# A two-layer decoder trunk on one core: ordering the whole program by a simulated timeline

## The chip, the core and the metric

The kernel runs on one core of a Trainium2 chip. It has a matrix engine (PE, whose weight loads are listed apart as PEld), a vector engine (DVE), a scalar engine (ACT), a general engine (POOL) and a queue that issues transfers (SP). Each engine works through its own list of instructions, and semaphores between the lists keep the data right. The metric is the time of one whole execution on the device in microseconds, the median of several runs.

## The reference

The input is one sequence of 512 tokens with 1024 channels, float32. Two layers each do a token mixer and a gated MLP, with a norm before each and a plain residual add; a last norm follows.

```python
def reference(x, ...):
    h = x
    for i in range(DEPTH):                       # DEPTH = 2
        hn = rms_norm(h, norm_mix[i])
        if i % N_MIXERS == 0:
            mix = pool_mixer(hn, pool_w[j], pool_b[j], pool_scale[j])
        else:
            mix = swa_sink_attention(hn, attn_w_qkv[j], attn_b_qkv[j], attn_sinks[j], attn_w_o[j])
        h = h + mix
        hn = rms_norm(h, norm_ffn[i])
        h = h + conv_glu_ffn(hn, ffn_w_in[i], ffn_conv_w[i], ffn_conv_b[i], ffn_w_out[i])
    return rms_norm(h, norm_f)
```

The pool mixer takes causal means over windows of 2, 4, 8 and 16 tokens, one window for each quarter of the channels, subtracts the token itself, and multiplies by one 256x256 matrix per quarter. The attention has 16 query heads of 64 over 4 key heads, a window of 128 tokens, a linear distance bias and one sink per head. The MLP goes from 1024 to 2x2816 channels, through a causal convolution of width 3 in each channel, multiplies one half by the silu of the other, and goes back to 1024.

## The kernel before

**Products.** Activations lie with channels on the 128 partitions and the 512 tokens along the row. Every product of the model is made three times on PE, from a rounded part (`_h`) and a rest (`_l`) of both factors: high by high (L84), high weight by low activation (L85), low weight by high activation (L86), in `mm3`. A weight tile is fetched by SP (L90, three raw buffers), rounded by a Copy on ACT (L98), and its rest is taken by a subtraction on DVE, in places on POOL (L101). There are four buffers each for `wh` and `wl`. PE adds up into eight banks, which are handed out in rings.

**Start, the pool mixer.** Tokens are squared on ACT (L268) and scaled on DVE (L270). 64 narrow matmuls with band matrices that POOL builds (L167 to L174) make the windowed means in all eight banks (L273). ACT reads a bank into `px_h` (L253), DVE takes the rest `px_l` (L254); this is `split_scaled`. Then come 48 products with the pool weights `wpool`. `h` arrives by transfer, gets a bias on ACT (L301) and the product on DVE (L307), and is split again into `f0x_h`, `f0x_l`, the input of the first MLP. Among the `px` splits the first MLP tiles, `wi_0_1`, `wi_0_0` and `wi_1_1`, get their Copy; their names give the index and the half of the gate.

**MLP.** Each MLP has two halves of 11 hidden tiles. `mlp_in` makes for each tile two banks of 24 matmuls, one for the value and one for the gate. The norm is not applied to the input; its reciprocal root is multiplied onto the product when DVE reads the bank (L315, `c_u`). So in the first half of each MLP the first banks wait for the norm. PE sums the squares (L232), DVE does the root, DVE puts it on a diagonal `n_d` (L242), PE spreads it over the partitions with a matmul by ones (L243), and ACT copies the result to `n_rb` (L246). Then follow the convolution (L318 to L320), silu (L344), the product `zz` (L347) and its split (L350, L351). `mlp_out` goes back by 33 matmuls for each of eight output tiles.

**Attention.** 16 units, one for each key head and block of 128 queries, go through scores (PE L556, DVE L559), the exponential (ACT L573), the scaling by the denominator (POOL L578), transposes (PE L586, split on ACT L589 and DVE L590) and the weighted values (PE L84 to L86 with `vh`, `vl`; split by ACT L605 and DVE L606). The source places fillers between these steps: the products of the later query tiles (`ax` by `kq`) and of the output projection (`o` by `wo`), at a set rate per unit.

**End.** The last norm is done in two token halves. The first half has its root spread by L243, copied (L246), and eight POOL multiplications (L689) make tiles `o` that SP sends out (L690). The second half is turned by PE (L664), its squares are summed (L699), and ACT and DVE scale four tiles `ob` (L715, L717) that SP sends out (L718).

**What sets the order.** The source is read once, and each instruction is recorded with what it depends on. A scheduler of the framework then makes each engine's list from this record. It chooses the next instruction by a model of the engines' times and respects the dependences, the buffers and the banks. The order in the source is only a starting point: where two instructions don't depend on each other they may stand either way round.

## Time and profile before

| | before |
|---|---|
| median of 3 runs | 929.1 us (928.81 to 929.13) |
| profiled execution | 929.16 us |
| its span | 927.4 us |
| granted PE clock, mean | 0.998 |
| PE busy | 913.8 us, 99% of the span |
| PEld busy | 770.3 us, 83% |
| DVE busy | 576.5 us, 62% |
| ACT busy | 423.3 us, 46% |
| POOL busy | 140.8 us, 15% |

The profile is of one execution. Rows of a timeline show the start, the duration, the engine, the line of the program, the operation, the output and its inputs, the shape, and in brackets how long the engine sat idle before it and what released it. Consecutive instructions of one kind on one engine stand in one row with their count. Matmuls are pipelined: the duration of one is longer than the distance from its start to the start of the next, and it is this distance that adds up.

### The profile page before, as it was taken

What the parts mean: (1) busy time and instruction counts of PE and PEld (TensorE: products, weight loads), DVE (VectorE), ACT (ScalarE), POOL (GpSimd) and SP (SyncE); (2) the same over time, 40 slices, a digit from 0 to 9 for tenths busy, and PEclk for the clock granted to TensorE, in tenths of its full rate; (3) what the DMA queues carried; (4) which work ended last, traced back from release to release, by engine and by line L of the source; (5) the groups of instructions that cost most, each with busy time, mean ns of one, the idle gap of its engine ahead of it and who ended that gap; (6) DMA issues with size and microseconds to landing.
All of it is one profiled execution on the core that took longest, in us unless ns stands there. A gap on an engine that the chain in (4) does not pass through costs nothing.

```text
span 927.4 us, 11708 instructions
## 1 busy us (share of the span) xinstructions
PE 913.8 (99%) x4419; PEld 770.3 (83%) x4419; DVE 576.5 (62%) x944; ACT 423.3 (46%) x682; POOL 140.8 (15%) x243
## 2 busy tenths in 40 slices
PE   8999999999999999999999999999999999999997
PEld 7788888888888888898888888888888888888896
DVE  5679776336777764455887472987743377677433
ACT  7655443223444443436887451744422244444532
POOL 9600000000000001227665140000000000000022
PEclk9999999999999999999999999999999999999999
DMA  9233222343222223322110041242233422322312
GB/s 332 70 113 114 91 86 76 97 128 111 94 92 93 77 77 98 133 92 91 47 46 24 18 142 51 86 150 95 63 94 100 136 91 93 110 80 63 96 61 91
DMA packets 28856, 88.14 MB, mean 95 GB/s; under 512 B 3200, under 2 KB 4352, under 8 KB 28800
## 3 DMA queue, kind: packets, MB, share of 16 engines
q1 hardware_dynamic: 28800, 87.40, 29.2%
q8 instruction: 34, 0.56, 0.3%
q14 instruction: 22, 0.18, 0.1%
HBM read 85.29 MB, written 2.10 MB: 94 GB/s over the span
## 4 chain that ended last, share of the span: by engine, by line
PE 91%; ACT 4%; DVE 2%; POOL 2%; issue 1%; ACTq 0%; POOLq 0%; DVEq 0%
PE bank L85 30%; PE bank L84 30%; PE bank L86 29%; ACT sc L573 1%; PE bank L556 1%; PE bank L586 1%; DVE tl L590 0%; ACT px_h L253 0%; POOL wo_l L101 0%; DVE q L469 0%; ACT th L589 0%; DVE sc L559 0%; PE bank L243 0%; ACT wi_h L98 0%; PE bank L273 0%
## 5 line engine op out<-in xcount | busy, mean ns | idle before, releaser
L226 POOL TENSOR_TENSOR n_acc<-n_acc,n_sq 128x512 f32<-128x512 f32 (+1 forms) x28 | 39.1, 1396 | 716.4 <-ACT n_sq L217 709.8
L98 ACT ACTIVATE wi_h<-wi_raw 128x1024 fp32r<-128x1024 f32 x88 | 92.9, 1060 | 109.1 <-PE bank L85 100.3
L85 PE MATMUL bank<-f0x_l,wi_h 128*128 128x512 f32 x352 | 137.1, 389 | 0.8 <-DVE f0x_l L254 0.8
L84 PE MATMUL bank<-f0x_h,wi_h 128*128 128x512 f32 x352 | 137.2, 390 | 0.0
L84 PE MATMUL bank<-f1x_h,wi_h 128*128 128x512 f32 x352 | 137.1, 390 | 0.0
L84 PE MATMUL bank<-zh,wo_h 128*128 128x512 f32 (+1 forms) x363 | 137.0, 378 | 0.0
L86 PE MATMUL bank<-f0x_h,wi_l 128*128 128x512 f32 x352 | 137.0, 389 | 0.0
L86 PE MATMUL bank<-f1x_h,wi_l 128*128 128x512 f32 x352 | 136.9, 389 | 0.0
L85 PE MATMUL bank<-f1x_l,wi_h 128*128 128x512 f32 x352 | 136.9, 389 | 0.0
L86 PE MATMUL bank<-zh,wo_l 128*128 128x512 f32 (+1 forms) x363 | 136.6, 376 | 0.0
L85 PE MATMUL bank<-zl,wo_h 128*128 128x512 f32 (+1 forms) x363 | 136.6, 376 | 0.0
L101 DVE TENSOR_TENSOR wi_l<-wi_raw,wi_h 128x1024 fp32r<-128x1024 f32 x84 | 102.7, 1225 | 48.9 <-ACT wi_h L98 37.2
L98 ACT ACTIVATE wo_h<-wo_raw 128x768 fp32r<-128x768 f32 (+1 forms) x70 | 57.5, 823 | 121.8 <-PE bank L85 109.9
L315 DVE TENSOR_TENSOR c_u<-bank,n_rb 128x512 f32<-128x512 f32 x88 | 60.0, 688 | 75.9 <-PE bank L86 75.9
L101 DVE TENSOR_TENSOR wo_l<-wo_raw,wo_h 128x768 fp32r<-128x768 f32 (+1 forms) x66 | 60.4, 915 | 54.5 <-ACT wo_h L98 54.3
L84 PEld LDWEIGHTS bank<-zh,wo_h 128*128 128x128 f32 x363 | 68.3, 188 | 12.4
L86 PEld LDWEIGHTS bank<-zh,wo_l 128*128 128x128 f32 x363 | 68.3, 188 | 12.3
L85 PEld LDWEIGHTS bank<-zl,wo_h 128*128 128x128 f32 x363 | 68.3, 188 | 12.3
L85 PEld LDWEIGHTS bank<-f0x_l,wi_h 128*128 128x128 f32 x352 | 66.1, 188 | 14.8 <-DVE f0x_l L254 1.2
L84 PEld LDWEIGHTS bank<-f0x_h,wi_h 128*128 128x128 f32 x352 | 66.1, 188 | 14.1 <-DVE h L307 0.4
L318 ACT ACTIVATE c_t<-c_u,vec 128x512 f32<-128x512 f32 x88 | 70.6, 811 | 15.4 <-DVE c_u L315 14.5
L86 PEld LDWEIGHTS bank<-f1x_h,wi_l 128*128 128x128 f32 x352 | 66.1, 188 | 13.8
(171 smaller groups left out, 1488.1 us busy)
## 6 DMA issues: line engine op xcount, KB each, us to landing
wi_raw<-w_in SPq DMA_DIRECT2D x88, 512.0 KB, 3.2
wo_raw<-w_out SPq DMA_DIRECT2D x31, 384.0 KB, 3.0
wo_raw<-w_out SPq DMA_DIRECT2D x31, 320.0 KB, 2.9
kq_raw<-w_kq SPq DMA_DIRECT2D x10, 512.0 KB, 3.3
wo_raw<-w_o SPq DMA_DIRECT2D x8, 512.0 KB, 3.3
xt<-x_tok SPq DMA_DIRECT2D x4, 512.0 KB, 5.2
h<-x_t SPq DMA_DIRECT2D x8, 256.0 KB, 7.6
wpool_raw<-w_pool SPq DMA_DIRECT2D x2, 512.0 KB, 8.1
```

Source lines behind the costliest of these rows:

```text
L84: T.matmul(ps, lhsT=wh, rhs=xh, start=start, stop=False, **kw)
L85: T.matmul(ps, lhsT=wh, rhs=xl, start=False, stop=False, **kw)
L86: T.matmul(ps, lhsT=wl, rhs=xh, start=False, stop=stop, **kw)
L98: A.activation(h[:, :n], raw[:, :n], AF.Copy)
L101: (eng or V).tensor_tensor(l[:, o], raw[:, o], h[:, o].bitcast(F32), ALU.subtract)
L226: eng.tensor_tensor(self.acc[:, lo:hi], self.acc[:, lo:hi], sq[:, lo:hi], ALU.add)
L315: V.tensor_tensor(u, ps, rb, ALU.mult)
L318: A.activation(t, u, AF.Identity, bias=col(V_CB + layer * 2 * NF + m), scale=cw[2])
L556: T.matmul(o, lhsT=qt, rhs=kt[:, kk : kk + 256], start=x == 0, stop=x == 1)
L573: A.activation(t, t, AF.Exp, bias=neg[:, i : i + 1], scale=-1.0, accum_out=den[:, i : i + 1])
L586: T.transpose(ps[:, i * P : (i + 1) * P], sc[i // 2][:, i % 2, kb * P : (kb + 1) * P], ident)
```

## The change

One argument is added where the program is opened. With it the scheduler chooses the next instruction by a simulation of the timeline of all engines, for the whole program, and not by its simpler model.

```diff
-    with tile.TileContext(nc) as tc:
+    with tile.TileContext(nc, schedule_with_timeline_sim=True) as tc:
         trunk(tc, *args, out_a, out_b)
```

No instruction is added or taken away; the lists hold the same work in another order. In the two lists 1069 rows of PE stand differently, 614 of DVE, 388 of ACT, 158 of POOL and 12 of SP. Three places follow.

The first is ACT's list in the pool mixer, as the difference between the two; `px_h` is the split of a bank of windowed means, `h_96` to `h_103` are the eight tiles of the residual, and the `wi` rows are Copies of MLP weights.

```order
 L286 ACTIVATE wpool_h<-wpool_raw 128x512 x4
 L98 ACTIVATE wi_0_1_h<-wi_0_1_raw 128x1024
+L98 ACTIVATE wi_0_0_h<-wi_0_0_raw 128x1024
+L98 ACTIVATE wi_1_1_h<-wi_1_1_raw 128x1024
 L253 ACTIVATE px_h<-bank_70,vec 128x512
+L301 ACTIVATE h_96<-h_96,bs 128x512
+L301 ACTIVATE h_97<-h_97,bs 128x512
 L253 ACTIVATE px_h<-bank_71,vec 128x512
 L253 ACTIVATE px_h<-bank_72,vec 128x512
+L301 ACTIVATE h_98<-h_98,bs 128x512
 L253 ACTIVATE px_h<-bank_73,vec 128x512
-L98 ACTIVATE wi_0_0_h<-wi_0_0_raw 128x1024
```

Two weight Copies now stand ahead of the first `px_h`, where they stood behind the fourth and the sixth, and two bias instructions stand between the first and the second `px_h`.

The second is PE's list in the first half of the first MLP, where the norm is spread (L243). Before, in a row:

```order
L84 MATMUL bank_70<-f0x_h,wi_2_1_h 128x512
L85 MATMUL bank_70<-f0x_l,wi_2_1_h 128x512
L86 MATMUL bank_70<-f0x_h,wi_2_1_l 128x512
L243 MATMUL bank_77<-n_d,ones 128x128 x4
L84 MATMUL bank_71<-f0x_h,wi_2_0_h 128x512
```

And now:

```order
L85 MATMUL bank_71<-f0x_l,wi_2_0_h 128x512
L86 MATMUL bank_71<-f0x_h,wi_2_0_l 128x512
L243 MATMUL bank_77<-n_d,ones 128x128 x4
L84 MATMUL bank_71<-f0x_h,wi_2_0_h 128x512
L85 MATMUL bank_71<-f0x_l,wi_2_0_h 128x512
L86 MATMUL bank_71<-f0x_h,wi_2_0_l 128x512
L84 MATMUL bank_72<-f0x_h,wi_3_1_h 128x512
```

Before, all 24 matmuls of `wi_2_0` stood between L243 and the first matmul that writes `bank_72` anew; now 3 of them do. `bank_72` holds the product of `wi_0_1` until `c_0_1_u` has been made from it with the spread norm. The first half of the second MLP is moved in the same way, from 24 matmuls to 3.

The third is PE's list in the second half of the attention. Before, in a row (`o` and `wo` are the output projection, `ax` and `kq` a query projection):

```order
L586 MATMUL bank_76<-ident,sc_3928 128x128 x2
L586 MATMUL bank_76<-ident,sc_3935 128x128 x2
L84 MATMUL bank_70<-ax_h,kq_h 128x512
L85 MATMUL bank_70<-ax_l,kq_h 128x512
L86 MATMUL bank_70<-ax_h,kq_l 128x512
L556 MATMUL bank_73<-kh_3815,q_0_3667 128x256
L556 MATMUL bank_73<-kl_3816,q_0_3667 128x256
L556 MATMUL bank_73<-kh_3815,q_1_3670 128x256
L556 MATMUL bank_73<-kl_3816,q_1_3670 128x256
L556 MATMUL bank_74<-kh_3815,q_0_3832 128x256
```

And now, in the same part of the list (the scores of a later unit, L556, follow the transposes, L586):

```order
L586 MATMUL bank_77<-ident,sc_3789 128x128 x2
L586 MATMUL bank_77<-ident,sc_3796 128x128 x2
L586 MATMUL bank_76<-ident,sc_3866 128x128 x2
L586 MATMUL bank_76<-ident,sc_3873 128x128 x2
L556 MATMUL bank_72<-kh_3815,q_0_3832 128x256
L556 MATMUL bank_72<-kl_3816,q_0_3832 128x256
L556 MATMUL bank_72<-kh_3815,q_1_3835 128x256
L556 MATMUL bank_72<-kl_3816,q_1_3835 128x256
L84 MATMUL bank_71<-th_3990,vh 128x256
L85 MATMUL bank_71<-tl_3991,vh 128x256
```

Between the transposes, the scores and the weighted values there is no filler now. All query projections are done 79 rows earlier in the list than before, and in the 161 rows behind the first six of the output projection, some seven units of the sixteen, 12 fillers stand in all, where six to twelve stood in each unit before.

At the end of the program two more things are moved. PE's L243 for the first token half of the last norm stood ahead of the 33 matmuls of the last output tile; now 24 of the 33 stand ahead of it and 9 behind. On SP, whose list held the eight transfers of `o` and then the four of `ob`, two of the four now stand ahead of the sixth and the eighth of the eight. At the start POOL fills and cuts the eight bands in another order, and PE does the band matmuls bank by bank and not token tile by token tile. The weight Copies of the MLPs' steady parts, the splits of the last hidden tiles and the narrow norm instructions change places with their neighbours in many rows.

## The prediction

> **What bounds the kernel now.** I read the page first, for the shares of the engines and the chain of work that ended last.
>
> ```profile
> PE 913.8 (99%) x4419; PEld 770.3 (83%) x4419; DVE 576.5 (62%) x944; ACT 423.3 (46%) x682; POOL 140.8 (15%) x243
> PEclk9999999999999999999999999999999999999999
> PE 91%; ACT 4%; DVE 2%; POOL 2%; issue 1%; ACTq 0%; POOLq 0%; DVEq 0%
> ```
>
> PE is busy for 913.8 of 927.4 us at full granted clock, and 91% of the chain that ended last is PE itself. So another order can't make the bulk faster; it can only fill or open PE's gaps. The table by stretches gives the size of PE's work. Its columns are the stretch, its length, then busy time and instructions of PE, PEld, DVE, ACT and POOL, the clock, the share of the DMA engines and GB/s.
>
> ```profile
> 60.00:100.00 40.00, 40.00 (x178) 33.11 (x178) 37.49 (x54) 23.67 (x31) 0.00 (x0) 1.00 0.32 103
> 430.90:532.80 101.90, 99.16 (x626) 87.79 (x625) 74.39 (x232) 75.54 (x217) 53.45 (x104) 1.00 0.12 39
> ```
>
> In the MLP's steady part PE makes 178 wide matmuls in 40.00 us, one in 0.225 us, without a gap; I use 0.227, the distance of two starts in the rows on the norm below. There the order of the other engines costs nothing unless it makes PE wait. The second row is the attention, to which I come back. PE's waits, from the view of waits (what waited, for whom, us in total, times, longest):
>
> ```profile
> PE bank L85 <- DVE tl L590: 1.0, 1, 1.0
> PE bank L85 <- DVE f0x_l L254: 0.8, 1, 0.8
> PE bank L84 <- ACT kh L452: 0.8, 1, 0.8
> PE bank L84 <- ACT oh L605: 0.8, 1, 0.8
> ```
>
> No wait is longer than about 1 us. There is little left to win, and a new order can lose at any place that has cover now. I therefore went through the lists at each place where something is moved across a matmul that needs it, and worked out the new starts by hand from the durations of this execution.
>
> **Start.** The rows of ACT, DVE and PE in the pool mixer, and the first three transfers of MLP weights (issues from 4.5 to 5.8 us, shortest, median and longest time to landing):
>
> ```profile
> L90 SPq DMA_DIRECT2D wi_raw<-w_in x3: 328/501/611, 4.5 to 5.8; - x3
> DMA to landing us min/median/max: 10.0/10.6/11.0
> 14.44 1.06 ACT L98 ACTIVATE wi_h<-wi_raw 128x1024 fp32r<-128x1024 f32 x1 [1.41 <-DMA wi_raw<-w_in]
> 15.56 2.43 ACT L253 ACTIVATE px_h<-bank,vec 128x512 fp32r<-128x512 f32 x4
> 22.04 1.99 ACT L301 ACTIVATE h<-h,bs 128x512 f32<-128x512 f32 x3
> 19.54 1.41 DVE L254 SCALAR_TENSOR_TENSOR px_l<-bank,vec,px_h 128x512 fp32r<-128x512 f32 x2 [0.54 <-ACT px_h L253]
> 28.10 0.39 PE L84 MATMUL bank<-f0x_h,wi_h 128*128 128x512 f32 x1
> 29.46 0.39 PE L84 MATMUL bank<-f0x_h,wi_h 128*128 128x512 f32 x1
> 30.67 0.50 PE L85 MATMUL bank<-f0x_l,wi_h 128*128 128x512 f32 x1 [0.82 <-DVE f0x_l L254]
> ```
>
> The third weight tile is issued at 5.8 and lands at about 16.8. Its Copy now stands ahead of the first `px_h`, and takes 1.06: the first `px_h` starts at 17.9 and not at 15.56. Four `px_h` take 2.43, about 0.6 each; so does a bias instruction (1.99 for three). Two of these now stand ahead of the second `px_h`, which ends at 17.9 + 4 x 0.6 = 20.4 or so. DVE adds 0.70 for `px_l`. PE's fifth product with the pool weights needs it, so it starts at 21.2, and 44 products are still to come: 44 x 0.227 = 10.0, and the first MLP matmul starts at 31.2, not at 28.10, 3.1 us later. Against that stands the gap from 29.46 to 30.67 and its small follower, 1.3 us beyond the normal distance, which the later start covers: by my walk `f0x_l` of the second tile is ready at 33.1, and is needed at 34.4. That makes 3.1 - 1.3 = **+1.8 us**. Bounds: +1.0, if only the first `px_h`'s delay of 2.3 counts, and +3.1, if a gap like today's opens again. POOL's other order of the bands delays the band matmuls to about 10.9 us, but by my walk they are through at 18.8, earlier than the second `px_h` is.
>
> The Trainium skill, in "PSUM — Partial Sum Buffer", section "Engine vs sequencer instructions", says that the queues of ScalarE, VectorE and GpSimd are strictly first in, first out. This rule speaks against the change: by it a `px_h` whose bank is complete can't pass a Copy that waits for its transfer, and the term is +1.8; if ACT could pass it, the term would be 0. The wait of 1.41 us in ACT's row above, with nothing of the `px_h` behind it started, agrees.
>
> **The norm's spread in the first halves of both MLPs.** PE and ACT at that place in the first MLP:
>
> ```profile
> 57.12 0.39 PE L85 MATMUL bank<-f0x_l,wi_h 128*128 128x512 f32 x1
> 57.34 0.39 PE L86 MATMUL bank<-f0x_h,wi_l 128*128 128x512 f32 x1
> 57.57 1.05 PE L243 MATMUL bank<-n_d,ones 128*128 128x128 f32 x8
> 58.38 0.48 PE L84 MATMUL bank<-f0x_h,wi_h 128*128 128x512 f32 x1
> 58.78 0.58 ACT L246 ACTIVATE n_rb<-bank 128x512 f32<-128x512 f32 x1
> 60.05 1.88 DVE L315 TENSOR_TENSOR c_u<-bank,n_rb 128x512 f32<-128x512 f32 x3
> ```
>
> Today 24 matmuls, 5.4 us, lie between L243 and the matmul that needs its bank emptied by the first `c_u`. Now it is 3. From the start of L243 at 57.57 its result is there after 1.05, at 58.62; `n_rb` takes 0.58 and the first `c_u` 0.63 to 0.69, with some 0.07 at each handing over (the last norm's rows below show it between ACT and POOL). PE can go on at 60.1. Its three matmuls start at 58.38 and are used up at 59.1. A wait of 1.0 opens, bounds 0.8 and 1.2; DVE and ACT are free there by their lists, since the Copy and the subtraction ahead are done during L243's delay. The second MLP has the same rows at the same place. **+2.0 us** together. The cover of DVE afterwards is thin (37.49 of 40 us in the first table row), but the later banks' deadlines are met by the walk, as each has 24 matmuls.
>
> **Attention.** The groups of instructions in the 101.9 us from the first scores to the last filler (busy time, mean ns of one | idle):
>
> ```profile
> L556 PE MATMUL bank<-kh,q 128*128 128x256 f32 x64 | 16.4, 287 | 0.0
> L586 PE MATMUL bank<-ident,sc 128*128 128x128 f32 x112 | 15.3, 272 | 0.0
> L84 PE MATMUL bank<-th,vh 128*128 128x256 f32 x56 | 15.9, 284 | 0.8 <-ACT kh L452 0.8
> L84 PE MATMUL bank<-ax_h,kq_h 128*128 128x512 f32 x40 | 16.5, 413 | 0.0
> L573 ACT ACTIVATE sc<-sc,neg 128x256 f32<-128x256 f32 (+1 forms) x64 | 30.1, 472 | 10.3 <-DVE neg L559 10.0
> L589 ACT ACTIVATE th<-bank 128x512 fp32r<-128x512 f32 x28 | 15.5, 591 | 0.4
> L605 ACT ACTIVATE oh<-bank 128x256 fp32r<-128x256 f32 x16 | 6.0, 373 | 8.6 <-PE bank L86 8.5
> L559 DVE CUSTOM_DVE_ANT_0 sc<-bank,dist,nsink 128x256 f32<-128x256 f32 (+1 forms) x64 | 25.6, 445 | 1.6 <-PE bank L556 1.5
> L590 DVE TENSOR_TENSOR tl<-bank,th 128x512 fp32r<-128x512 f32 x28 | 18.4, 685 | 1.3 <-ACT th L589 1.0
> ```
>
> Per unit (sixteen, on average) PE's own steps are 8 L556 at 0.12 (the distance of such narrow matmuls), 7 L586 at 0.11 and 10.5 weighted products at 0.12, about 3.0 us. ACT's are (30.1 + 15.5 + 6.0) / 16 = 3.2, with small ones 3.4; DVE's (25.6 + 18.4) / 16 = 2.8, with `ol` and the denominator 3.5. All 626 matmuls at their normal distances (218 wide ones at 0.227 make 49.5, the rest 47.5) come to 97.0 us of the 101.9, so 4.9 us are gaps and slow restarts today. The fillers are what lets PE run on while ACT and DVE are slower than it.
>
> The new list takes query projections out of the later units. For some seven units PE's work of 3.0 us per unit, with 12 wide fillers in all, stands against 3.5 of DVE and 3.4 of ACT: 7 x 0.5 = 3.5 us are lost less what the 12 fillers cover. At the end, behind the last weighted product, 4 matmuls of the output projection stand where 12 stood, so the last `oh` and `ol` show: 1.1 by a walk. In the walk of the whole stretch the four long waits of today go, others on L559's banks and on `tl` come, and it ends 0.1 us later than before. I add 0.9 for restarts behind these waits, as each costs about 0.1 in today's rows: **+1.0 us**. Bounds: all of today's 4.9 gone against 3.2 lost, -1.7; nothing gone, 3.7 + 1.1 lost, +4.8. I take a value near the lower middle, since the walk has every instruction in it and the bounds don't.
>
> **End.** The rows of the last norm's first half, whose L243 is now behind 24 of the 33 last matmuls:
>
> ```profile
> 914.41 0.61 PE L243 MATMUL bank<-n_d,ones 128*128 128x128 f32 x4
> 915.06 0.39 ACT L246 ACTIVATE n_rb<-bank 128x256 f32<-128x256 f32 x1 [3.57 <-PE bank L243]
> 915.20 0.28 PE L85 MATMUL bank<-zl,wo_h 128*128 128x256 f32 x1
> 915.32 0.28 PE L86 MATMUL bank<-zh,wo_l 128*128 128x256 f32 x1
> 915.52 5.83 POOL L689 TENSOR_TENSOR o<-hg,n_rb 128x256 f32<-128x256 f32 x8 [7.11 <-ACT n_rb L246]
> 916.29 5.43 SPq L690 DMA_DIRECT2D out_a<-o  x8
> 922.67 1.95 SPq L718 DMA_DIRECT2D out_b<-ob  x4
> ```
>
> 24 matmuls at 0.12 and the turn that stood behind make 3.1 us, so `n_rb` comes at 918.2 and POOL's eight run from 918.6 to 924.4. Today they end at 921.35, and SP sends the four `ob` from 922.67 to 924.62. In the new list the last `o` is sent ahead of the last two `ob`: at 924.4, and then two issues of about 0.4. The last one starts at 925.1 and not at 924.2, **+0.9 us**. Bounds: +0.6, if POOL is through sooner, and +2.0, if its last tiles meet SP late.
>
> **At nothing.** The swaps at the passage from `mlp_in` to `mlp_out` (the last hidden tile's three matmuls moved back), of Copies and subtractions among weights in the steady parts and of L232 are covered by whole tiles of 24 or 33 matmuls, 5.4 us and more. If that cover were gone at one place it would cost a Copy and a subtraction, 1.06 and 1.23 at most.
>
> **Sum.** 1.8 + 2.0 + 1.0 + 0.9 = 5.7 on the profiled execution's 929.16 makes 934.9; that execution lies 0.06 above the median, so **934.8 us**. The low ends of the terms (1.0, 1.6, -1.7, 0.6) give 1.5 and 930.6, the high ends (3.1, 2.4, 4.8, 2.0) give 12.3 and 941.4.
>
> **The rivals.** *The bare units run at the pace of the softmax chain.* If ACT needs what it needs today per unit with all its copies, 75.54 / 16 = 4.7 us, because Copies for the output projection still stand between, seven units lose 7 x 1.7 = 12 us, less the 4.9 of today's gaps: +7 in place of +1.0, 941. For it speaks that ACT and DVE are at 75% and 73% there already; against it, that the chains of three units overlap. The Trainium skill, in "Perfetto Trace Analysis", section "Optimization Strategy", advises interleaving regimes whose most loaded engine differs; taking the fillers away from the units undoes this, and by that rule this rival is the likelier. No row here has bare units.
>
> *The attention gains more than the rest loses.* Moving the query projections forward gives ACT and DVE their queries early, and the softmax runs ahead of PE. Then all of the 4.9 us goes and no bare unit costs anything: 929.16 + 1.8 + 2.0 - 4.9 + 0.9 = 929.0, not slower. It decides from a gain of 2.8 us in the attention on, as the other terms make 4.7 and a measurement of this kernel can't tell 0.2%, 1.9 us, from no change. For it speaks that the waits on `tl`, `kh` and `oh` are the longest ones of the kernel; against it, that PE needs 3.0 us per unit and DVE 3.5.
>
> *The order doesn't bind.* If the moved instructions find what they need ready anyway, as most of the 1069 rows do, the time is 929. It would need the weights to land by 14.5 and the spread norm to be there without L243; I see no way for either.
>
> **How the numbers follow.** My forecast has 0.70, the bare units 0.12, the attention's gain 0.12, the order that doesn't bind 0.06. Slower by over 0.2% (above 931.0) are the forecast, but for its lowest part, and the bare units: 0.81. No change gets 0.13 and faster 0.06, from the last two and that lowest part. The range of 930.0 to 940.5 leaves out the worst of the bare units and the attention's full gain.
>
> **What would show it.** Right would be: the first `px_h` near 17.9 us and the first MLP matmul near 31; a new wait of PE at L84 for `c_u` of L315, twice, about 1 us each; no long wait for `kh`, and PE waiting for `tl` and L559 in the second half of the attention; POOL's last `o` past 924 counted from the old start of the end. Wrong would be a first MLP matmul at 28 to 29, no wait for `c_u`, or an attention shorter than 99 us or longer than 106.

## The result and the profile after

The changed kernel takes 939.9 us (median of four executions: 947.97, 939.85, 939.9 and 939.3) where the kernel before took 928.95 beside it on the same chip: a ratio of 1.0136, 95% interval 1.0117 to 1.0155; the medians alone give 1.0118. It is slower. Two executions of all the runs here were at a granted clock of 0.556 (1549.7 us, one of four in the run that puts the attention's lists of before into the change, and 1542.95, one of the kernel before beside it) and are left out. The profiled execution happened to be the one of 947.97; what held it for 8 us more is told in the last section. The same kernel was therefore profiled once more (the first experiment below), in an execution of 939.13 us with a span of 937.4, and everything between here and there is read from that profile. Against the 927.4 us of the span before, it is 10.0 us longer.

The page of the second profile, the shares of the engines:

```profile
PE 917.4 (98%) x4419; PEld 772.6 (82%) x4419; DVE 581.5 (62%) x944; ACT 423.2 (45%) x682; POOL 140.6 (15%) x243
```

The same numbers of instructions, and on DVE 5.0 us more of busy time for the same 944. PE's busy time has grown by 3.6 us only; the rest of the 10 us are gaps. PE's waits:

```profile
PE bank L273 <- POOL band L174: 4.6, 1, 4.6
PE bank L84 <- DVE ol L606: 1.4, 2, 0.8
PE bank L84 <- DVE c_u L315: 1.4, 2, 0.7
PE bank L586 <- DVE tl L590: 1.1, 3, 0.4
PE bank L556 <- DVE neg L559: 0.7, 2, 0.3
```

The waits on `kh`, on `f0x_l` and the one of 1.0 us on `tl` are gone. New are `c_u` of L315 twice, which the prediction named, and `ol` of L606 twice, which it did not. The wait on the bands is at the very start; its cost is judged by when the first MLP matmul starts.

Four places in PE's list give the account. Each time but the last is PE's start of the same matmul in the two profiles:

| PE's start of | before | after | later by | since the place above | forecast |
|---|---|---|---|---|---|
| first MLP matmul | 28.10 | 31.76 | 3.66 | 3.66 | 3.1 |
| first product of `mlp_out` of the first MLP | 150.95 | 154.30 | 3.35 | -0.31 | -0.3 (-1.3 for the gap, 1.0 for L243) |
| last product of `mlp_in` of the second MLP | 855.35 | 863.16 | 7.81 | 4.46 | 2.0 (1.0 attention, 1.0 L243) |
| end of the span | 927.42 | 937.42 | 10.00 | 2.19 | 0.9 |

**Start.** The rows of PE and ACT in the pool mixer, and PE's first MLP matmul:

```profile
10.93 10.10 PE L273 MATMUL bank<-band,xt 128*128 128x144 f32 x64 [4.62 <-POOL band L174]
16.57 1.06 ACT L98 ACTIVATE wi_h<-wi_raw 128x1024 fp32r<-128x1024 f32 x1 [0.17 <-DMA wi_raw<-w_in]
18.03 0.69 ACT L253 ACTIVATE px_h<-bank,vec 128x512 fp32r<-128x512 f32 x1 [0.40 <-PE bank L273]
19.84 1.25 ACT L253 ACTIVATE px_h<-bank,vec 128x512 fp32r<-128x512 f32 x2
```

The first `px_h` starts at 18.03 and the second one ends near 20.5, both within 0.15 us of the forecast's 17.9 and 20.4. But the Copies didn't hold the first one: ACT's third weight Copy was through at 17.63, and by the bracket ACT then sat idle for 0.40 us until PE had the first bank. The 64 band matmuls take 10.10 us and are through at 21.03, not at 18.8. The reason is the clock. Here are first a row of the kernel before, and then two stretches of the band matmuls in the change, with the columns of the prediction's first table:

```profile
12.58 4.50 PE L273 MATMUL bank<-band,xt 128*128 128x144 f32 x36 [0.35 <-POOL band L170]
11.00:15.00 4.00, 4.00 (x17) 4.00 (x18) 1.93 (x3) 2.78 (x5) 4.00 (x8) 0.50 1.03 416
16.00:20.00 4.00, 4.00 (x36) 4.00 (x35) 0.75 (x1) 3.43 (x6) 4.00 (x4) 1.00 1.05 404
```

PE waited for POOL's bands from 6.3 to 10.93 us. From 8.55 to 15.38 the trace has a granted clock of 0.50, and in that time PE starts a band matmul every 0.24 us; behind it every 0.12, as in the kernel before, where the clock stays at 1.00. 18 matmuls at 0.12 us more are 2.2 us, which is what lies between 18.8 and 21.03. So none of the 48 products was made ahead of that; the first starts at 20.78, and 48 x 0.227 = 10.9 later comes 31.7. The second `px_l` alone would have let it start at the forecast's 31.2; the late bands add 0.5.

**The norm's spread.** PE, ACT and DVE behind L243 in the first MLP:

```profile
65.77 0.60 ACT L246 ACTIVATE n_rb<-bank 128x512 f32<-128x512 f32 x1 [4.36 <-PE bank L243]
66.03 0.40 PE L86 MATMUL bank<-f0x_h,wi_l 128*128 128x512 f32 x1
66.40 1.89 DVE L315 TENSOR_TENSOR c_u<-bank,n_rb 128x512 f32<-128x512 f32 x3 [3.73 <-ACT n_rb L246]
67.14 0.50 PE L84 MATMUL bank<-f0x_h,wi_h 128*128 128x512 f32 x1 [0.71 <-DVE c_u L315]
```

The third matmul starts at 66.03, so the next could start at 66.26; it starts at 67.14, 0.88 later, and its own start-up adds less than 0.1. That is the walk's 1.0, twice.

**Attention.** The first two rows of the table by stretches of the two kernels, before first, with its columns as in the prediction:

```profile
430.90:475.00 44.10, 42.11 (x262) 36.91 (x261) 36.74 (x119) 37.72 (x109) 30.53 (x57) 1.00 0.18 61
475.00:503.00 28.00, 28.00 (x192) 25.27 (x191) 21.52 (x70) 22.27 (x68) 16.96 (x34) 1.00 0.12 39
```

```profile
434.20:478.50 44.30, 44.30 (x266) 39.23 (x266) 35.77 (x102) 36.21 (x95) 31.42 (x55) 1.00 0.22 72
478.50:512.00 33.50, 31.00 (x211) 26.63 (x210) 27.16 (x99) 27.85 (x92) 17.25 (x39) 1.00 0.06 17
```

The end's stretch follows (503 to 533 and 512 to 536). Before, PE idled in the first stretch, where the softmax isn't filled yet, and ran without a gap in the middle. After, the first stretch, where the query projections now stand, has no gap, and the middle one idles. To have it in one figure I took each distance between two starts of PE's matmuls less the normal one (0.227, 0.12 or 0.11 us by their width) and summed: before 3.2, 0.6 and 1.1 us are lost in the three stretches, 5.0 in all; after 0.1, 6.1 and 2.2, 8.5 in all. The difference is 3.5, which is the 4.46 of the table above less the second wait for `c_u`.

Where a bare unit loses time is seen in the timeline of DVE and PE, and in the busy times from one `ol` to the next (PE, PEld, DVE, ACT, POOL):

```profile
485.68 0.42 DVE L606 TENSOR_TENSOR ol<-bank,oh 128x256 fp32r<-128x256 f32 x1
486.16 0.39 PE L84 MATMUL bank<-th,vh 128*128 128x256 f32 x1 [0.85 <-DVE ol L606]
487.88 0.69 DVE L590 TENSOR_TENSOR tl<-bank,th 128x512 fp32r<-128x512 f32 x1 [0.61 <-ACT th L589]
489.69 0.42 DVE L606 TENSOR_TENSOR ol<-bank,oh 128x256 fp32r<-128x256 f32 x1
493.67 0.39 PE L556 MATMUL bank<-kh,q 128*128 128x256 f32 x1 [0.32 <-DVE neg L559]
493.94 0.42 DVE L606 TENSOR_TENSOR ol<-bank,oh 128x256 fp32r<-128x256 f32 x1
489.69:493.94 4.25, 3.92 (x30) 3.34 (x30) 3.69 (x16) 3.66 (x13) 2.05 (x5) 1.00 0.00 0
```

The weighted values of every unit go to one bank (L595; the ring `av` has one). PE may write it again only when `oh` and `ol` have read it. `oh` is there at 488.28, but `ol` starts at 489.69: DVE's list puts a `tl` and three score rows (L559) ahead of it. From `ol` to `ol` it is 4.0 and 4.25 us in the units without any filler, where the walk gave a bare unit 3.5. No engine is full in them: in the one from 489.69 DVE is busy for 3.69 us and ACT for 3.66, and PE's matmuls at their normal distances make 3.3. Who waited for L606, by the view of that line (total us, times), in the stretch from 478 to 540 after:

```profile
  PE bank L84: 1.4, 2
```

Before, the same view lists nobody: the fillers stood behind the weighted values and `ol` was long done. But `ol` is only one of three. In the middle stretch PE waits 0.85 us for it, 0.76 for `tl` and 0.9 for the score rows of L559, all results of DVE. The chain of work that ended last goes through `ol` once (486.16), through `tl` twice, and through the score rows ahead of PE's L556 at 489.43, 493.67, 499.06, 506.79 and 511.04.

**End.** DVE's rows at the end before, and then the rows of POOL and DVE after:

```profile
921.41 0.22 DVE L202 SCALAR_TENSOR_TENSOR rs_t<-rs_y,rs_v 128x1 f32<-128x1 f32 x1
921.71 0.15 DVE L206 SCALAR_TENSOR_TENSOR n3b_r<-rs_t,rs_y 128x1 f32<-128x1 f32 x1
```

```profile
926.48 5.52 POOL L689 TENSOR_TENSOR o<-hg,n_rb 128x256 f32<-128x256 f32 x8 [10.20 <-ACT n_rb L246]
929.28 0.68 DVE L202 SCALAR_TENSOR_TENSOR rs_t<-rs_y,rs_v 128x1 f32<-128x1 f32 x1
929.99 0.65 DVE L206 SCALAR_TENSOR_TENSOR n3b_r<-rs_t,rs_y 128x1 f32<-128x1 f32 x1
931.34 0.66 DVE L202 SCALAR_TENSOR_TENSOR rs_t<-rs_y,rs_v 128x1 f32<-128x1 f32 x1
932.04 0.16 DVE L206 SCALAR_TENSOR_TENSOR n3b_r<-rs_t,rs_y 128x1 f32<-128x1 f32 x1
```

Three instructions on a single column take 0.65 to 0.68 us in place of 0.15 to 0.22. All three lie inside POOL's eight multiplications, and the fourth, just behind POOL's end at 932.00, takes 0.16 again. They are on the path from the last matmul to `ob`, and cost 1.4 us together. Each ends within 0.03 us of the end of one of the eight, which follow each other every 0.68 us: it waits for the one that runs. SP's order makes about the rest. Its last issue ends at 934.77, 1.79 us behind the last `ob`; before it was 924.62, 0.87 behind. That is 0.9 more, the forecast's figure.

### The profile page after: what moved, and what is told of

It reads as the page before. It is cut to its first block, busy times and chain, and to the rows that moved or that the text cites. A ratio compares the mean times of both kernels' runs of the same rounds, so it can differ in the third digit from the quotient of the medians.

```text
span 946.2 us, 11719 instructions
## 1 busy us (share of the span) xinstructions
PE 918.2 (97%) x4419; PEld 772.9 (82%) x4419; DVE 592.8 (63%) x944; ACT 422.5 (45%) x682; POOL 139.9 (15%) x243
## 4 chain that ended last, share of the span: by engine, by line
PE 94%; DVE 3%; ACT 1%; DMA 0%; issue 0%; ACTq 0%; DVEq 0%
PE bank L84 30%; PE bank L86 30%; PE bank L85 30%; PE bank L556 2%; DVE r L206 1%; PE bank L586 1%; DVE rs_t L202 1%; PE bank L273 1%; DMA xt<-x_tok 0%; DVE sc L559 0%; DVE xt L270 0%; ACT th L589 0%; PE bank L243 0%; PE bank L232 0%; ACT sc L573 0%
## 5 line engine op out<-in xcount | busy, mean ns | idle before, releaser
L226 POOL TENSOR_TENSOR n_acc<-n_acc,n_sq 128x512 f32<-128x512 f32 (+1 forms) x28 | 39.3, 1402 | 717.6 <-ACT n_sq L217 710.8
L84 PE MATMUL bank<-f1x_h,wi_h 128*128 128x512 f32 x352 | 137.1, 390 | 0.7 <-DVE c_u L315 0.7
L84 PE MATMUL bank<-f0x_h,wi_h 128*128 128x512 f32 x352 | 136.3, 390 | 0.7 <-DVE c_u L315 0.7
L84 PE MATMUL bank<-zh,wo_h 128*128 128x512 f32 (+1 forms) x363 | 136.4, 377 | 0.0
L315 DVE TENSOR_TENSOR c_u<-bank,n_rb 128x512 f32<-128x512 f32 x88 | 59.9, 688 | 78.9 <-PE bank L86 71.6
L84 PEld LDWEIGHTS bank<-zh,wo_h 128*128 128x128 f32 x363 | 68.3, 188 | 12.3
L84 PEld LDWEIGHTS bank<-f0x_h,wi_h 128*128 128x128 f32 x352 | 66.1, 188 | 14.7 <-DVE c_u L315 1.2
L84 PEld LDWEIGHTS bank<-f1x_h,wi_h 128*128 128x128 f32 x352 | 66.1, 188 | 14.7 <-DVE c_u L315 1.2
```

The lines of the kernel that those rows point to most:

```text
L84: T.matmul(ps, lhsT=wh, rhs=xh, start=start, stop=False, **kw)
L226: eng.tensor_tensor(self.acc[:, lo:hi], self.acc[:, lo:hi], sq[:, lo:hi], ALU.add)
L315: V.tensor_tensor(u, ps, rb, ALU.mult)
```

## The experiments

The edits change the order of instructions and nothing else, unless it is said. `behind(a, b)` records that a stands behind b, `mark` and `traced` pick the instructions that one engine got since a place in the source, `chain` holds them in the order of the source, and `replay` in that of a given list. These helpers stand at the top of the kernel, so lines are 19 or 25 higher in most rows here (L84 is L103 or L109), and up to 33 in the last trial.

**The change again.** The kernel as it is.

> The changed kernel once more, nothing edited. In the profile taken with the result DVE held one tiny instruction of the pool mixer (L206, 128x1, normally 0.2 us) for 9.5 us, exactly until a row of five POOL instructions was through, and PE waited 8.1 us for it; the other three executions were 8.1 us shorter. If this hold is a matter of a few hundredths of a microsecond at one boundary between POOL instructions: most executions near 939.6, L206 under 3 us in the profile, PE's longest wait at L273 under 5 us, and first MLP matmul near 32.5. If the hold belongs to the order: every profile has it, and the time is 948.

939.75 us (939.13 to 939.88), ratio 1.0113 (1.0096 to 1.0130), beside 929.24 for the kernel before. No execution was near 948; this is the typical profile shown above.

**The attention's order on PE from the source.**

```diff
+        m1 = mark()
...
+        chain(m1, ET.PE)
```

> The changed kernel, but PE's list in the attention is held to the order of the source (fillers between the units), by edges that set the order on PE alone. If the thinned-out units cost what the trace shows between the first scores and the end of the output projection (3.9 us more than before): 939.6 - 3.9 = 935.7. If the loss there comes from what DVE, ACT and POOL do in their new order: 939 to 940.

941.88, 954.82, 954.7 and 942.48 us, ratio 1.0207 (1.0135 to 1.0278): worse than the change, and neither expectation. The profile of 941.88 shows other waits in the place of the old ones:

```profile
PE bank L575 <- DVE q L488: 2.6, 2, 2.3
PE bank L104 <- DVE tl L609: 2.5, 2, 2.3
```

One engine's list, put back alone, doesn't fit the lists of the others, which still make `q` and `tl` for the new order. The executions of 955 have no trace; what they lost is open.

**L243 early in both MLPs.** The 24 matmuls of the next product stand behind the last L243.

```diff
+            if spr:
+                behind(traced(m0, ET.PE), spr.pop())
...
+                spr.append(traced(m0, ET.PE)[-1])
```

> The changed kernel, but PE's L243 is held ahead of the 24 matmuls of wi_2_0 in the first half of both MLPs. If each of the two waits for c_u is on the path (0.9 us in the trace): 939.6 - 1.8 = 937.8, and no wait for c_u at L84. If PE's wait only moves on to the next bank: 939 to 940.

939.12 us (937.83 to 939.5), ratio 1.0104: 0.6 less than the change, not 1.8, and within the spread of its own executions. The two waits for `c_u` are gone, and another has come:

```profile
PE bank L262 <- DVE n_d L261: 0.9, 2, 0.5
```

DVE's list makes `n_d` for the later place, so L243 itself now waits for it. This shows the wait for `c_u` to come from the place of L243, and not that the loss can be had back by moving PE alone.

**L243 of the last norm early.** All 33 matmuls of the last tile stand behind it.

```diff
+            if m == NC - 1:
+                behind(traced(m0, ET.PE), spr3)
...
+                spr3 = traced(m0, ET.PE)[-1]
```

> The changed kernel, but the last norm's L243 is held ahead of the last output tile's 33 matmuls, which also puts SP's transfers back nearly as they were. The end from PE's last matmul is 8.7 us against 6.6 before. If L243 alone makes this: 939.6 - 2.1 = 937.5. If the forecast's 0.9 is what L243 makes, and the rest has another cause: 938.7.

937.65 us (937.17 to 937.96), ratio 1.0090: 2.1 less than the change, as expected. From the start of DVE's last L653 to the end of the span it is 8.20 us, as in the kernel before (8.19; in the change 10.33): the end's loss hangs on this one place. That the total fits to a tenth is in part chance: PE loses 0.65 us at the early L243, which waits for `n_d`, and this execution's first MLP matmul was 0.55 us earlier, at 31.21.

**The attention's lists of before, on all engines, in the changed kernel.**

```diff
+        m1 = mark()
...
+        replay(m1, mark(), {"PE": [3080, 3081, ...
```

> The changed kernel, but in the attention the lists of PE, DVE, ACT and POOL are held to those of before, row by row, by edges that set the order alone. If the attention's new order costs what the trace shows between the first scores and the last product of the output projection (3.9 us): 939.6 - 3.9 = 935.7, with that stretch back at 164 us from the first query product on. If the loss depends on what comes ahead of it or behind it: 938 to 940.

935.03, 935.2 and 935.19 us, ratio 1.0064 (1.0047 to 1.0081): 4.5 less than the change, 1.0 more than the attention loses in the table. The only trace of this run is one of those left out, so where the 4.5 lie isn't shown.

**The attention's lists of the change in the kernel before.** The same edit with the other lists.

> The kernel before, but in the attention the lists of the four engines are held to those of the changed kernel. The same question from the other side. If the order there costs 3.9 by itself: 929.1 + 3.9 = 933.0. The forecast's +1.0: 930.1. If the new order only fits the changed kernel's start: more than 934.

932.68 us (932.28 to 932.74), ratio 1.0037 (1.0022 to 1.0051): +3.5, the size that the table gives. Its waits hold the new ones of the change, of which the kernel before has none for `ol` and one for `tl`:

```profile
PE bank L109 <- DVE ol L632: 1.4, 2, 0.8
PE bank L612 <- DVE tl L616: 1.3, 4, 0.4
```

The lost time of PE, summed as above, is 0.1, 6.1 and 2.2 us in the three stretches, like that of the change. So the attention's lists make its loss by themselves.

**The Copies first, in the kernel before.** Two weight Copies ahead of the first `px_h`, two bias instructions ahead of the second.

```diff
+                if c in (3, 5):
+                    behind(px_a[0], traced(m0, ET.Activation)[0])
...
+            if c < 2:
+                behind(px_a[1], traced(m0, ET.Activation)[0])
```

> The kernel before, but on ACT the Copies of wi_0_0 and wi_1_1 are held ahead of the first px_h, and two bias instructions ahead of the second. The forecast's first term alone: first px_h near 17.9 us, second through at 20.4, +1.8 us, 930.9, bounds +1.0 and +3.1. If POOL's order of the bands is what delays the start in the changed kernel: 929 to 929.5.

932.34 us (932.13 to 932.89), ratio 1.0034 (1.0021 to 1.0048): +3.1. ACT and PE there:

```profile
18.05 0.67 ACT L278 ACTIVATE px_h<-bank,vec 128x512 fp32r<-128x512 f32 x1
19.56 0.71 PE L109 MATMUL bank<-px_h,wpool_h 128*128 128x512 f32 x1 [2.91 <-DVE px_l L279]
```

The first `px_h` is where the forecast put it, at 18.05, and here the Copies hold it: all bands were through at 16.65. The first MLP matmul starts at 32.23, 4.1 us late. PE had waited 2.91 us for `px_l`; from 19.68 to 23.09 the granted clock was 0.50, and products stood 0.43 us apart, not 0.227. The fifth product starts at 21.35, so at full clock the other 44 would have been through at 31.3, the forecast's 31.2; I estimate the half clock at the remaining 0.9. The term of 1.8 is too small here, and its upper bound of 3.1 is met. This shows that the Copies are enough to make such a loss, and not that they made it in the change, where PE waited for bands instead. POOL's order of the bands was not tried alone.

**L243 late in both MLPs, in the kernel before.** L243 behind 21 of the 24.

```diff
+            if spr:
+                behind(spr.pop(), traced(m0, ET.PE)[20])
```

> The kernel before, but PE's L243 is held behind 21 of the 24 matmuls of wi_2_0 in the first half of both MLPs, as in the changed kernel. The forecast's second term alone: one wait for c_u of about 0.9 us in each MLP, 929.1 + 2.0 = 931.1, bounds 930.7 and 931.5. If part of each wait is had anyway (the changed kernel's second MLP is only 0.6 us longer than the one before): 930.3.

940.94 us (940.83 to 942.17), ratio 1.0131: +11.8, far more than either expectation. The waits:

```profile
PE bank L111 <- DVE wi_l L126: 6.1, 2, 3.1
PE bank L109 <- DVE c_u L340: 1.4, 2, 0.7
```

The wait for `c_u` is the same 1.4 in two as in the change, so its size is confirmed. But the scheduler, given this one rule, also moved DVE's list, and two weight rests came 3 us late. Behind each of these two waits the granted clock was 0.50 for 3.4 us, with products 0.43 us apart, which I estimate at 1.6 us each. The total isn't that of the one step.

**L243 of the last norm late, in the kernel before.** Behind 24 of the 33.

```diff
+            if m == NC - 1:
+                behind(spr3, traced(m0, ET.PE)[23])
```

> The kernel before, but the last norm's L243 is held behind 24 of the last output tile's 33 matmuls. The forecast's fourth term alone, the later transfers: +0.9, 930.0. If the DVE instructions of the second half's root are held by POOL's multiplications that now run beside them (0.68, 0.65 and 0.66 us in the changed kernel's trace for what takes 0.21 to 0.22 alone): +2.1 or a little more, 931.2, with those three rows near 0.65 again.

930.85 us (930.62 to 931.12), ratio 1.0020 (1.0010 to 1.0029): +1.75. Of this 1.4 us are POOL holding DVE's small instructions, and 0.4 SP's order, whose last issue ends 1.28 us behind the last `ob`. DVE's rows, while POOL's eight multiplications run from 918.34 to 923.85:

```profile
921.13 0.68 DVE L227 SCALAR_TENSOR_TENSOR rs_t<-rs_y,rs_v 128x1 f32<-128x1 f32 x1
921.85 0.65 DVE L231 SCALAR_TENSOR_TENSOR n3b_r<-rs_t,rs_y 128x1 f32<-128x1 f32 x1
923.20 0.66 DVE L227 SCALAR_TENSOR_TENSOR rs_t<-rs_y,rs_v 128x1 f32<-128x1 f32 x1
```

The same three durations as in the change, in a kernel in which only this place was moved.

**A weight rest on DVE, in the kernel before.** The rest of `wi_1_0` made by DVE and not POOL, to see whether POOL makes the old gap at `f0x_l`.

```diff
-                ws.append(in_weights(0, *pre[c // 2], G, raws[c // 2]))
+                ws.append(in_weights(0, *pre[c // 2], G if c < 7 else V, raws[c // 2]))
```

> The kernel before, but the rest of the fourth MLP weight tile, wi_1_0, is taken on DVE and not on POOL; the lists of PE, ACT and SP stay the same. Before, f0x_l of the second tile takes 2.75 us on DVE beside this POOL instruction, for 0.75 alone, and PE has a gap of 1.3 us behind it. If POOL's instruction holds the DVE one: f0x_l 0.75 again, the gap gone, 929.1 - 1.0 to 1.3 = 928.0. If f0x_l is slow by itself: 929 or, for the 1.2 us more on DVE, above.

929.04 us, ratio 0.9999 (0.9990 to 1.0008): no change. `f0x_l` was held again, by the next thing that POOL did, an addition:

```profile
28.51 1.44 POOL L226 TENSOR_TENSOR n_acc<-n_acc,n_sq 128x512 f32<-128x512 f32 x1 [0.80 <-ACT n_sq L217]
28.72 1.77 DVE L254 SCALAR_TENSOR_TENSOR f0x_l<-h,vec,f0x_h 128x512 fp32r<-128x512 f32 x1
```

**The rest and the additions on DVE, in the kernel before.** The last experiment, and the additions of the first norm's squares (L226) moved from POOL to DVE too.

```diff
+                ws.append(in_weights(0, *pre[c // 2], G if c < 7 else V, raws[c // 2]))
...
-            norm.add(c)
+            norm.add(c, eng=V)
```

> The kernel before, but the rest of wi_1_0 and the seven additions of squares (L226) in the pool mixer are on DVE and not on POOL. With the rest alone moved, f0x_l of the third tile was held by an addition instead, 1.77 us for 0.75, and the gap stayed. If any POOL instruction with two inputs holds it, and now none runs: f0x_l 0.75, the gap of about 1 us gone, 928.0, faster than both kernels. If DVE's 6 us more of work come late somewhere else: 929 to 930.

928.29 us (927.83 to 928.55), ratio 0.9990 (0.9982 to 0.9999), 0.9 us less than the kernel before. `f0x_l` takes 0.75 us, where it took 2.75 before:

```profile
28.38 0.75 DVE L279 SCALAR_TENSOR_TENSOR f0x_l<-h,vec,f0x_h 128x512 fp32r<-128x512 f32 x1
```

So the gap of 1.2 us at the start, which the prediction set down to a late `f0x_l`, was DVE held by POOL. Of all kernels here this one is the fastest, by the width of a measurement.

**Three trials on the 8 us of the first profile.** In the first, three DVE instructions of 128x1024 stand ahead of the last small one of the tokens' norm; in the second, two, with the lists otherwise as in the change; in the third, 1.5 us more of squares stand ahead of ACT's first one, so that all of DVE's starts later.

```diff
+            for _ in range(3 if late is not None else 0):
+                V.tensor_scalar(late, late, y, None, ALU.mult)
```

```diff
+            for _ in range(2 if late is not None else 0):
+                V.tensor_scalar(late, late, y, None, ALU.mult)
```

```diff
+        A.activation(late[:, :D], xt[:, 0, :], AF.Square)
+        A.activation(late[:, D:], xt[:, 0, :512], AF.Square)
```

> The changed kernel with three more DVE instructions (128x1024 on a tile that nothing reads, about 2.2 us together) ahead of the last L202 of the pool mixer, which pushes it and the L206 behind it from 10.7 us into POOL's run of seven subtractions (12.4 to 24.6). If a DVE instruction with two SBUF inputs waits only for the POOL instruction that is running (2.4 us at most each): two or three such waits, +3 to +5, 943 to 945, in every execution. If it is held until POOL's run is through, as in the first profile: L206 done past 24 us, +8 to +9, 948 in every execution.

> The changed kernel with two more DVE instructions of 128x1024 (1.5 us) ahead of the last L202 of the pool mixer, so that L202 comes near 12.2 us as in the first profile of the changed kernel; the rest of DVE's list is that of the changed kernel. With three of them and one tiny instruction more in between, nothing was held past the next boundary of POOL's instructions. If the timing of L202 and L206 against that boundary decides: L206 held till past 24 us in some or all executions, 948. If the first profile's hold had another cause: 939.5 to 941 in all.

> The changed kernel with 1.5 us more on ACT (two squares of a token tile into a tile that nothing reads) ahead of the first square of the pool mixer. This makes the last L202 and L206 on DVE late against POOL's run of subtractions, as in the first profile of the changed kernel, without any more DVE work that would hold POOL back in turn. If POOL's run holds the tiny DVE instructions to its end once it is ahead: L206 or L202 held till past 22 us, first MLP matmul past 38, 947 or more in most executions. If each is held for the running POOL instruction alone: L206 done by 17 us, 939.5 to 941.5.

939.5, 939.1 and 939.63 us: like the change, in each of the twelve executions. The second tests nothing: its small instructions were through at 12.60, ahead of POOL's subtractions at 13.42. In the first, POOL's pair of rests took 3.40 us and not 2.49, while DVE's long instructions ran beside it. In the third, the small instructions met POOL's run in full:

```profile
12.53 5.44 POOL L320 TENSOR_TENSOR wpool_l<-wpool_raw,wpool_h 128x512 fp32r<-128x512 f32 x4 [0.83 <-ACT wpool_h L318]
12.79 1.04 DVE L227 SCALAR_TENSOR_TENSOR rs_t<-rs_y,rs_v 128x1 f32<-128x1 f32 x1
13.87 1.20 DVE L231 SCALAR_TENSOR_TENSOR r<-rs_t,rs_y 128x1 f32<-128x1 f32 x1
```

Each was held until the POOL instruction that was running ended, about 1.2 us, and then had its turn. A hold over several POOL instructions did not come again.

## Why the prediction was right and wrong

The direction was right, for the reason given: PE had cover that the old order used, and the new one takes some of it away at the four places named. The typical loss is 10.6 us against 5.7 forecast; the four terms forecast 5.7 and measure 10.0 in the two profiles. Three steps failed: the pace of the bare units in the attention, which cost most, DVE beside POOL at the end, and the speed of the band matmuls at the start.

**Start, 1.8 forecast, 2.4 measured** (3.66 less the 1.26 that the old gap gave back). The number is near by luck. The step that failed is "by my walk they are through at 18.8": from 10.9 to 18.8 the walk gave each of the 64 band matmuls 0.12 us, and so it put POOL's new order of the bands at nothing. In PE's wait of 4.62 us for the bands the granted clock went to 0.50, where it stayed until 15.38; the first 18 took 0.24 each, and the last was through at 21.03. All 48 products came behind that, not 44. So in the change the late bands set the start; the Copies alone would have let PE start at the forecast's 31.2, by the second `px_l`, and are hidden by 0.5 us. That they can make the loss is shown in the kernel before (+3.1).

The prediction read ACT's wait of 1.41 us before as agreeing with the Trainium skill's rule on in-order queues ("PSUM — Partial Sum Buffer", section "Engine vs sequencer instructions"). That row couldn't show it, since no bank was complete until 15.3. The run with the Copies first does agree: there ACT waited 0.17 us for the third transfer, up to 17.08, when every bank had been through since 16.65.

**Spread of the norm, 2.0 forecast, 1.9 measured.** The walk from L243 over `n_rb` and the first `c_u` to PE's fourth matmul is confirmed to a tenth, in the change and again where L243 was moved late in the kernel before.

**Attention, 1.0 forecast, 3.5 measured.** This is the term that failed by most. The prediction priced two things well: today's gaps in the first part go (3.2 to 0.1 us), and the end shows the last `oh` and `ol` (1.1 to 2.2, the walk's 1.1). The step that failed is that a bare unit is paced by DVE's work of 3.5 us, "7 x 0.5 = 3.5 us are lost less what the 12 fillers cover". The units without filler took 4.0 to 4.25, and the middle lost 5.5 us more than before (0.6 to 6.1). The sum of an engine's durations per unit is a lower bound, and here it wasn't reached: DVE was busy for 3.2 to 3.7 us of these units. PE, ACT and DVE wait for each other in turn, and PE each time for a result of DVE (`ol`, `tl` or a score row) that stands behind work for another unit in DVE's list. In the order of before, a filler stood there. That the lists cause the loss is shown twice, by putting them into the kernel before (+3.5) and taking them out of the change (-4.5). Which of the three waits decides is not shown: no run moved one of them alone or gave the weighted values a second bank.

The rival of bare units at 4.7 us had the right place and too high a price, and its reason, ACT, isn't what the rows show: ACT is busy for 2.9 to 3.7 us in these units. Its total of 941 is near the measured one only because the other terms were too small. The rule of the Trainium skill that stood behind it ("Perfetto Trace Analysis", section "Optimization Strategy": performance may improve by interleaving regimes whose most loaded engine differs) agrees in direction with the two runs on the lists, and 0.12 was too little for it.

**End, 0.9 forecast, 2.2 measured.** The walk of POOL holds: its last `o` ends at 932.00, and 7.81 us earlier, in the time of the kernel before, that is 924.2, against 924.4 forecast. So does the 0.9 for SP's order. The step that failed is one put at nothing: POOL's eight now run beside the small instructions of the second half's norm, three of these are held by POOL, and that adds 1.4 us. Moving L243 back in the change makes the end as short as before, and moving it late in the kernel before costs 1.75, with the three durations of 0.65 to 0.68.

**At nothing.** That the swaps elsewhere in the two MLPs cost nothing holds in the traces: between the places in the table no difference is left that isn't named. The moves in the kernel before (3.1, 3.5 and 1.75) and the two waits for `c_u` (1.9) make 10.3 of the 10.6, but that sum is no proof: the 3.1 has another cause than the change's 2.4 at the start.

Each of the marks named in the prediction came: `px_h` near 18, the first MLP matmul near 31 (31.76), `c_u` twice, no wait for `kh`, waits for `tl` and L559, and POOL past 924. That they came, and the time was still 5 us off, shows that such marks test whether a step happens, and not what it costs. The first came for another reason than the one given: a mark should be read with what released it.

## What to carry to other kernels

When a new order takes fillers away from a chain over several engines, price a bare round by walking it from engine to engine, with what stands ahead of each step in its engine's list, and not by the busiest engine's sum: here it took 4.0 to 4.25 us, not 3.5. Where an order makes PE wait longer than before, look at the granted clock behind the wait. When a list moves a run of POOL work in time, look for what DVE does beside it, however small. And an order is made for all engines together: put back on one engine it gained nothing here, put back on four it gained 4.5 us.

## What the runs showed of the hardware

A DVE instruction with two inputs from the SBUF was held by the POOL instruction that ran: on a single column 0.65 to 1.2 us in place of 0.15 to 0.22, and 2.75 in place of 0.75 for `f0x_l`. The Trainium skill says so ("SBUF — State Buffer", section "Who interferes with whom": the second to issue is blocked until the first finishes), and the rows above agree. Beside the same POOL run at the end, the reciprocal of L190, with one input, took its usual 0.15. Two rows that don't agree are in the first profile of the change, the execution of 947.97 us:

```profile
12.05 2.49 POOL L287 TENSOR_TENSOR wpool_l<-wpool_raw,wpool_h 128x512 fp32r<-128x512 f32 x2
12.19 2.37 DVE L202 SCALAR_TENSOR_TENSOR rs_t<-rs_y,rs_v 128x1 f32<-128x1 f32 x1
14.59 9.50 DVE L206 SCALAR_TENSOR_TENSOR r<-rs_t,rs_y 128x1 f32<-128x1 f32 x1
14.69 2.49 POOL L287 TENSOR_TENSOR wpool_l<-wpool_raw,wpool_h 128x512 fp32r<-128x512 f32 x2
17.15 6.93 POOL L101 TENSOR_TENSOR wi_l<-wi_raw,wi_h 128x1024 fp32r<-128x1024 f32 x3
24.94 0.58 PE L273 MATMUL bank<-band,xt 128*128 128x128 f32 x1 [8.13 <-DVE xt L270]
```

One instruction on 128 single values lasted 2.37 us, through two of POOL's instructions, and the next one 9.50 us, through five POOL instructions back to back, and ended when POOL's run did; PE waited 8.13 us for the tokens behind it, which is the difference of 8 us to the typical execution. So the wait can outlast the instruction that runs. In the 19 other executions of the change and of the three trials it didn't return (none took over 940.2 us); the two executions of 955 us have no trace. What decides it is open.

PE's granted clock was at 0.50 behind some of its waits. In the two profiles of the change and in the six traces at full clock of trials in it, it was 0.50 for 3.4 or 6.8 us around the wait for the bands (4.62 us in the typical profile). With 3.4 us the first MLP matmul was at 31.05 and 31.21 in the two trials on L243, with 6.8 at 31.76 in the change. In the kernel before, where no wait is longer than 1.2 us, it stayed at 1.00 up to PE's last matmul.
